# Short convolutions of a hybrid DeltaNet block: the sigmoid goes into the copied block, squares are summed on ScalarE, the halo comes from PSUM

## The chip, the cores and the metric

The kernel runs on one core of one Trainium2 chip. The metric is the device time of one execution in microseconds (us), the median of three runs. Five engines work beside each other, each through its own instructions in order: PE (TensorE, the matmuls; PEld is its weight loading), DVE (VectorE), ACT (ScalarE), POOL (GpSimd) and SP (SyncE, which issues nearly all DMAs). They wait for each other by semaphores.

## The reference

One layer of a hybrid encoder on x of 2048 tokens by 1024 channels, all in float32. One input projection feeds a gated DeltaNet (branch A) and stick-breaking attention (branch B); both are projected up, gated, merged and projected out. The change touches branch A's short causal convolution and the L2 norms of q and k:

```python
proj = jnp.einsum('bsd,dp->bsp', xn, w_in)                   # xn: RMS-normalised x
qkv_a = silu(_causal_dwconv(proj[..., :A_QKV1], conv_w))     # 4 taps along the tokens, per channel
q_a = _l2n(qkv_a[..., :nqk]...)                              # x * rsqrt(sum(x*x) + EPS), 4 heads of 128
k_a = _l2n(qkv_a[..., nqk:2*nqk]...)
v_a = qkv_a[..., 2*nqk:]
o_a = _gated_delta_rule(q_a, k_a, v_a, g, beta)              # chunks of 64 tokens, 128x128 states
...
o_b = _stick_breaking(q_b, k_b, v_b)                         # strictly causal, 8 heads of 64
merged = gates_a * (o_a @ w_up_a) + gates_b * (o_b @ w_up_b)
return x + merged @ w_out
```

## The kernel before

The projection runs unit by unit: a unit is a group of columns of w_in, for all tokens. Weights and normalised x are both held as a rounded part and a remainder (whi, wlo and xh, xl), and a product takes three matmuls per 128-row slice of the 1024 inputs, so 24 matmuls of 128x512 make one block of 128 channels by 512 tokens (`mm_chan`, L384 to L394). The block lies in PSUM under the name pj; there are four such banks.

The units come in this order: the gate path z of branch A, then the convolutions, then the projections of branch B with the triangular solves in between, then attention among the remaining projections, and the recurrence and the output products at the end. The stage of the convolutions is the stretch from about 124 to 490 us. It has four units of q and k, one per head, and two units of v. A q/k unit runs over four groups of 512 tokens, and in each over k's block and q's block (s = 0 and 1; called a pair below): 16 pairs. The v units have 16 blocks, one after the other.

Each block passes through `conv` (L534). ACT copies it from PSUM to a tile u of 515 columns (L542), whose first three columns are the last three of the block before (the halo, L541; zeros at the start, L539). DVE takes the halo for the next block (L544), multiplies the block by one tap (L546, a TENSOR_SCALAR) and adds the other three taps with three SCALAR_TENSOR_TENSOR in place on acc (L548). ACT makes the sigmoid of acc in a tile sg (L550), and POOL multiplies acc by sg, into kq for q and k (L565) or in place for v (L631).

Three steps after a pair, `qk_tok` (L572) follows it up: PE transposes k's and q's chunks to PSUM tiles tp (L582), ACT squares each of them to a tile sq (L584), DVE sums the squares by row (L585) and copies k's transposed tile (tk, L588), and a few small operations make the norms (L591 to L599, partly on POOL). POOL builds two masked tiles gm (L578), PE multiplies them to the sums of the decay exponents, ACT takes their Exp in a tile e (L605), and POOL masks e and makes en from it (L606, L610). One step later `gram` (L608) has PE make the products of k with k and q, and DVE multiplies them by en and e (L616, L617). The sigmoid and Exp need different function tables on ACT, hence the ACT_TABLE_LOADs on L550 and L605.

All tiles named u, acc, sg, gm, sq, tk, e and en come from one ring of seven buffers (tag "a", `self.na`, L212): a new tile takes the buffer of the tile seven allocations earlier and waits until its readers are done. The next unit's weights arrive in halves: ACT rounds a half (L329) and POOL takes the remainder (L330).

The program is written in the order of the loops, but a scheduler with its own timeline places the instructions of each engine, so what stands in front of what on an engine is not seen in the source.

Of the kernel before, what the change touches and what calls it, by code (L numbers as in the profile page):

```python
# [9 lines left out]
BF16 = mybir.dt.bfloat16  # L10
F32R = mybir.dt.float32r
I32 = mybir.dt.int32
AF = mybir.ActivationFunctionType
ALU = mybir.AluOpType
AX = mybir.AxisListType
# [3 lines left out]
P = 128  # L19
# [4 lines left out]
TG = 512  # L24
NG = S // TG
NH = 4
# [11 lines left out]
class Block:  # L38
# [156 lines left out]
    def stage1(self):  # L195
# [9 lines left out]
        with ExitStack() as ctx:  # L205
            with ExitStack() as early:
                self.pj = early.enter_context(self.pool("pj", bufs=4, space=PSUM))
                self.pt = early.enter_context(self.pool("pt", bufs=4, space=PSUM))
                self.wp = early.enter_context(self.pool("wp", side="right"))
                self.wcols, self.nraw = 264, 1  # L210
                with self.pool("wka", side="right") as self.wk:
                    self.na, self.nb = 7, 5  # L212
                    self.prep = self.prep_x(za[0][1])
                    next(self.prep)
                    self.units(za + conv, sb[0])
                    self.flush()
                self.wk = early.enter_context(self.pool("wkb", side="right"))
                self.na, self.nb = 8, 1
                with self.pool("sv", side="right") as self.sv:
                    self.back, self.credit = self.dn_solve(), 0.0  # L220
                    self.rate = 2.7
                    self.units(sb[:-1], sb[-1])
                    self.drain()
                wide = self.wp
                self.wp = ctx.enter_context(self.pool("wpc"))
                self.wcols = P
                self.units(sb[-1:], zb[0])
                self.flush()
# [305 lines left out]
    def conv(self, ps, b, halo):  # L534

        nc = self.nc
        u = self.a([P, TG + 3], "u")
        if halo is None:
            nc.vector.memset(u[:, 0:3], 0.0)  # L539
        else:  # L540
            nc.vector.tensor_copy(u[:, 0:3], halo)  # L541
        nc.scalar.copy(u[:, 3:], ps)  # L542
        halo = self.wk.tile([P, 3], F32, tag="halo", name="halo", bufs=4)
        nc.vector.tensor_copy(halo, u[:, TG:TG + 3])  # L544
        acc = self.a([P, TG], "acc")
        nc.vector.tensor_scalar(acc, u[:, 3:], self.tap(3, b), None, ALU.mult)  # L546
        for k in range(3):
            nc.vector.scalar_tensor_tensor(acc, u[:, k:k + TG], self.tap(k, b), acc, ALU.mult, ALU.add)  # L548
        sg = self.a([P, TG], "sg")
        nc.scalar.activation(sg, acc, AF.Sigmoid)  # L550
        return acc, sg, halo

# [19 lines left out]
    def qk_tok(self, kq, tg, h):  # L572

        nc, wk = self.nc, self.wk
        cs = slice(4 * tg, 4 * tg + 4)
        gm = [self.a([P, 4, P], "gm", F32R) for _ in range(2)]
        for t, g in zip(gm, (self.g_hi, self.g_lo)):
            nc.gpsimd.tensor_tensor(t, self.tri_le.unsqueeze(1).to_broadcast([P, 4, P]), self.col(g, tg, h).to_broadcast([P, 4, P]), ALU.mult)  # L578
        for s, ssq in ((0, self.ssq_k), (1, self.ssq_q)):
            pt = self.pt.tile([P, 4, P], F32, tag="tp", name="tp")  # L580
            for c in range(4):
                self.tr(pt[:, c], kq[:, c, s], self.ident)  # L582
            sq = self.a([P, 4, P], "sq")
            nc.scalar.activation(sq, pt, AF.Square)  # L584
            nc.vector.tensor_reduce(self.col(ssq, tg, h), sq, AX.X, ALU.add)  # L585
            if s == 0:
                tk = self.a([P, 4, P], "tk")
                nc.vector.tensor_copy(tk, pt)  # L588
                nc.sync.dma_start(self.d_kt[cs, :, h].rearrange("c p d -> p c d"), tk)
        v = wk.tile([P, 2, 4, 1], F32, tag="nv", name="nv")  # L590
        nc.vector.tensor_scalar(v[:, 0], self.col(self.ssq_k, tg, h), EPS, None, ALU.add)  # L591
        nc.vector.tensor_scalar(v[:, 1], self.col(self.ssq_q, tg, h), EPS, None, ALU.add)
        r = wk.tile([P, 4, 1], F32, tag="nr", name="nr")
        nc.vector.reciprocal(r, v[:, 0])
        nbr = self.col(self.nbr, tg, h)
        nc.vector.scalar_tensor_tensor(nbr, r, -1.0, self.col(self.beta, tg, h), ALU.mult, ALU.mult)
        nc.vector.tensor_tensor(self.col(self.nbe, tg, h), nbr, self.col(self.ed, tg, h), ALU.mult)
        nc.gpsimd.tensor_tensor(self.col(self.nk, tg, h), v[:, 0], self.half[:, 0:4].unsqueeze(2), ALU.pow)
        nc.gpsimd.tensor_tensor(self.col(self.rq, tg, h), v[:, 1], self.mhalf[:, 0:4].unsqueeze(2), ALU.pow)  # L599

        ps = self.pt.tile([P, 4, P], F32, tag="tp", name="tp")
        for k in (1, 0):
            self.mm(ps.rearrange("p c i -> p (c i)"), self.tri_gt, gm[k].rearrange("p c i -> p (c i)"), start=k == 1, stop=k == 0)
        e = self.a([P, 4, P], "e")
        nc.scalar.activation(e, ps, AF.Exp)  # L605
        nc.gpsimd.affine_select(e, e, pattern=[[0, 4], [1, P]], compare_op=ALU.is_ge, fill=0.0, base=0, channel_multiplier=-1)  # L606

        def gram():  # L608
            en = self.a([P, 4, P], "en")
            nc.gpsimd.tensor_tensor(en, e, nbr.to_broadcast([P, 4, P]), ALU.mult)  # L610
            for c2 in range(2):
                ps = self.pt.tile([P, 2, 2, P], F32, tag="tp", name="tp")
                cc = slice(2 * c2, 2 * c2 + 2)
                for c in range(2):
                    self.mm(ps[:, c], kq[:, 2 * c2 + c, 0], kq[:, 2 * c2 + c], start=True, stop=True)
                nc.vector.tensor_tensor(en[:, cc], ps[:, :, 0], en[:, cc], ALU.mult)  # L616
                nc.vector.tensor_tensor(e[:, cc], ps[:, :, 1], e[:, cc], ALU.mult)  # L617
            nc.sync.dma_start(self.d_mt[cs, h].rearrange("c j i -> j c i"), en)
            nc.sync.dma_start(self.d_qk[cs, :, h].rearrange("c j i -> j c i"), e)

        self.defer(1, gram)
# [499 lines left out]
```

## Time and profile before

| | |
|---|---|
| median of three runs | 2125.48 us (2123.26 to 2127.56) |
| the profiled execution | 2125.88 us, of which 2124.2 us is the span from the first to the last instruction |
| busy over the span | PE 2057.2 us (97%), PEld 1826.7 (86%), DVE 1408.6 (66%), ACT 878.0 (41%), POOL 932.3 (44%) |
| granted TensorE clock, mean | 0.994 |
| the chain that ended last | PE 37%, DVE 5%, DMA 4%, ACT 2%, issue 2%, POOL 1% |

PE is busy nearly all the time, so the places where it is not are what other engines cost. Matmuls are pipelined: a 128x512 matmul is shown with some 0.4 us, while such matmuls start 0.23 us apart. A row of the timeline that has a bracket at its end tells how long the engine had been idle before the instruction and what it was waiting for.

### The profile page before, as it was taken

How to read it: one execution, taken by the hardware profiler on the slowest of the kernel's cores; microseconds unless marked ns; L12 is line 12 of the kernel's file. 1: busy time of each engine (PE TensorE's matmuls, PEld its weight loads, DVE VectorE, ACT ScalarE, POOL GpSimd, SP SyncE). 2: the span in 40 equal slices, each digit the busy share in tenths (PEclk: the TensorE clock that was granted, in tenths of full speed). 3: DMA queues.
4: the chain of work that ended last, by engine and by line, in shares of the span. 5: the costliest groups of instructions: out<-in, count | busy, mean ns of one | idle time of the engine just before them, and what ended most of it. 6: DMA issues, size and time to landing. Idle time of an engine off the chain costs nothing.

```text
span 2124.2 us, 36554 instructions
## 1 busy us (share of the span) xinstructions
PE 2057.2 (97%) x12903; PEld 1826.7 (86%) x12903; DVE 1408.6 (66%) x2579; ACT 878.0 (41%) x1695; POOL 932.3 (44%) x1140
## 2 busy tenths in 40 slices
PE   8999988999999999999999999999999999999999
PEld 7988766779999988888888888888888899999887
DVE  7357787887998418887888887778744466433221
ACT  6233344322222116666666666766633321211110
POOL 4336666633443105555555554555537555521000
PEclk9999999999999999999999999999999999999999
DMA  7223333226333653444574443333346787764442
GB/s 240 63 63 95 95 95 94 85 70 120 105 120 101 159 147 103 114 117 118 148 185 122 130 122 100 109 110 108 97 133 211 234 264 220 228 189 137 152 139 80
DMA packets 279702, 282.52 MB, mean 133 GB/s; under 512 B 49440, under 2 KB 215520, under 8 KB 279392
## 3 DMA queue, kind: packets, MB, share of 16 engines
q1 hardware_dynamic: 279520, 280.19, 45.1%
q8 instruction: 103, 1.69, 0.3%
q14 instruction: 79, 0.65, 0.1%
HBM read 177.35 MB, written 102.76 MB: 132 GB/s over the span
## 4 chain that ended last, share of the span: by engine, by line
PE 37%; DVE 5%; DMA 4%; ACT 2%; issue 2%; POOL 1%; SPq 0%; DVEq 0%; ACTq 0%; POOLq 0%
PE pj L124 9%; PE o L124 8%; PE y L124 7%; PE dn L124 4%; PE av L124 3%; PE at L128 3%; DVE r L1068 2%; PE z L124 2%; DMA wraw<-in_w_in_dram 2%; DVE lo L1088 1%; ACT z L1066 1%; ACT s L1065 1%; DMA raw<-in_w_out_dram 0%; POOL xl L880 0%; DMA raw<-in_w_up_a_dram 0%
## 5 line engine op out<-in xcount | busy, mean ns | idle before, releaser
L1072 POOL TENSOR_TENSOR s<-s,r 128x512 f32<-128x512 f32 (+2 forms) x320 | 306.1, 957 | 336.8 <-DVE r L1068 330.6
L124 PE MATMUL pj<-xh,whi 128*128 128x512 f32 x1024 | 421.4, 411 | 12.2 <-ACT u L542 10.3
L124 PE MATMUL pj<-xh,wlo 128*128 128x512 f32 x1024 | 405.7, 396 | 0.0
L124 PE MATMUL pj<-xl,whi 128*128 128x512 f32 x1024 | 405.3, 396 | 0.0
L124 PE MATMUL pj<-whi,xh 128*128 128x256 f32 (+1 forms) x1024 | 294.4, 288 | 0.9 <-ACT xh L380 0.9
L124 PE MATMUL pj<-whi,xl 128*128 128x256 f32 (+1 forms) x1024 | 290.7, 284 | 0.0
L124 PE MATMUL pj<-wlo,xh 128*128 128x256 f32 (+1 forms) x1024 | 290.5, 284 | 0.2 <-DVE wlo L330 0.2
L1068 DVE TENSOR_TENSOR_SCAN r<-z,carry,zero 128x512 f32<-128x512 f32 x192 | 245.8, 1280 | 65.7 <-ACT z L1066 60.3
L124 PEld LDWEIGHTS pj<-xh,whi 128*128 128x128 f32 x1024 | 194.2, 190 | 49.4 <-ACT u L542 15.1
L124 PEld LDWEIGHTS pj<-xh,wlo 128*128 128x128 f32 x1024 | 193.7, 189 | 44.6
L1065 ACT ACTIVATE s<-z 128x512 f32<-128x512 f32 (+2 forms) x320 | 171.4, 536 | 133.4 <-PE z L124 53.6
L124 PEld LDWEIGHTS pj<-xl,whi 128*128 128x128 f32 x1024 | 194.6, 190 | 31.8
L1088 DVE TENSOR_TENSOR lo<-at,hi 128x512 fp32r<-128x512 f32 (+1 forms) x288 | 182.8, 651 | 27.2 <-ACT hi L1087 25.9
L124 PEld LDWEIGHTS pj<-whi,xh 128*128 128x128 f32 x1024 | 195.4, 191 | 1.3 <-ACT xh L380 1.3
L124 PEld LDWEIGHTS pj<-wlo,xh 128*128 128x128 f32 x1024 | 195.6, 191 | 0.5 <-DVE wlo L330 0.5
L124 PEld LDWEIGHTS pj<-whi,xl 128*128 128x128 f32 x1024 | 195.0, 191 | 0.3 <-DVE xl L381 0.3
L124 PE MATMUL z<-kt,qt 128*128 128x512 f32 (+3 forms) x640 | 189.0, 376 | 0.4 <-DVE r L1068 0.2
L1087 ACT CAST hi<-at 128x512 fp32r<-128x512 f32 (+1 forms) x288 | 154.0, 566 | 85.0 <-PE at L128 82.5
L330 POOL TENSOR_TENSOR wlo<-wraw,whi 128x512 fp32r<-128x512 f32 (+2 forms) x66 | 116.5, 1765 | 129.6 <-ACT whi L329 127.4
L1066 ACT ACTIVATE z<-z 128x512 f32<-128x512 f32 (+2 forms) x320 | 170.8, 534 | 0.1
L548 DVE SCALAR_TENSOR_TENSOR acc<-u,cols,acc 128x512 f32<-128x512 f32 x144 | 154.6, 1073 | 5.0
L128 PE MATMUL at<-ident,s 128*128 128x128 f32 x1088 | 155.6, 275 | 1.8 <-POOL s L1072 1.4
(200 smaller groups left out, 4285.3 us busy)
## 6 DMA issues: line engine op xcount, KB each, us to landing
kt<-d_k SPq DMA_DIRECT2D x160, 128.0 KB, 3.0
vt<-d_v SPq DMA_DIRECT2D x80, 256.0 KB, 3.6
xt<-in_x_dram SPq DMA_DIRECT2D x32, 512.0 KB, 3.6
qt<-d_q SPq DMA_DIRECT2D x64, 256.0 KB, 5.4
d_g<-sg SPq DMA_DIRECT2D x128, 128.0 KB, 2.5
gt<-d_g SPq DMA_DIRECT2D x64, 256.0 KB, 3.5
wraw<-in_w_in_dram SPq DMA_DIRECT2D x56, 256.0 KB, 3.3
wraw<-in_w_in_dram SPq DMA_DIRECT2D x18, 512.0 KB, 3.9
```

Source lines behind the costliest of these rows:

```text
L124: self.pin(self.nc.tensor.matmul(out, lhsT, rhs, **kw))
L128: self.pin(self.nc.tensor.transpose(*args))
L330: (eng or nc.gpsimd).tensor_tensor(lo[:, ks, :n], raw[:, :, :n], hi[:, ks, :n].bitcast(F32), ALU.subtract)
L548: nc.vector.scalar_tensor_tensor(acc, u[:, k:k + TG], self.tap(k, b), acc, ALU.mult, ALU.add)
L1065: nc.scalar.activation(s[:, :w], z[:, :w], AF.Sigmoid, scale=SD ** -0.5)
L1066: nc.scalar.activation(z[:, :w], z[:, :w], AF.Sigmoid, scale=-(SD ** -0.5))
L1068: nc.vector.tensor_tensor_scan(r[:, 0:w][:, ::-1], z[:, 0:w][:, ::-1], self.zero.to_broadcast([P, w]), init, ALU.mult, ALU.add)
L1072: nc.gpsimd.tensor_mul(s[:, :w], s[:, :w], r[:, 1:w + 1])
L1087: nc.scalar.copy(hi[:, c:], flat[:, c:])
L1088: nc.vector.tensor_tensor(lo[:, c:], flat[:, c:], hi[:, c:].bitcast(F32), ALU.subtract)
```

## The change

Three edits, all in `conv` and `qk_tok`. The sigmoid is written over the first 512 columns of u, so that sg no longer takes a buffer of the ring. The halo for the next block is copied from the block in PSUM and no longer from u. And each transposed tile is squared chunk by chunk, four ACT operations of 128x128, whose row sums go to the norm's columns directly; the squares themselves go to a bfloat16 tile sink that nobody reads. The tile sq and DVE's two sums fall away. The ring serves 9 tiles per pair and no longer 13.

```diff
@@ conv
         nc.scalar.copy(u[:, 3:], ps)
         halo = self.wk.tile([P, 3], F32, tag="halo", name="halo", bufs=4)
-        nc.vector.tensor_copy(halo, u[:, TG:TG + 3])
+        nc.vector.tensor_copy(halo, ps[:, TG - 3:TG])
...
-        sg = self.a([P, TG], "sg")
+        sg = u[:, 0:TG]
         nc.scalar.activation(sg, acc, AF.Sigmoid)
@@ qk_tok
-            sq = self.a([P, 4, P], "sq")
-            nc.scalar.activation(sq, pt, AF.Square)
-            nc.vector.tensor_reduce(self.col(ssq, tg, h), sq, AX.X, ALU.add)
+            junk = wk.tile([P, P], BF16, tag="sink", name="sink", bufs=1)
+            for c in range(4):
+                n = NH * (4 * tg + c) + h
+                nc.scalar.activation(junk, pt[:, c], AF.Square, accum_out=ssq[:, n:n + 1])
```

The scheduler places the instructions anew in the whole stage. On ACT, one round of a q/k pair in the middle of the stage stands like this before (u are the copied blocks, sg the sigmoids, e the Exp):

```order
L542 COPY u<-pj 128x512
L550 ACT_TABLE_LOAD
L550 ACTIVATE sg<-acc 128x512
L542 COPY u<-pj 128x512
L550 ACTIVATE sg<-acc 128x512
L584 ACTIVATE sq<-tp 128x512 x2
L605 ACT_TABLE_LOAD
L605 ACTIVATE e<-tp 128x512
L542 COPY u<-pj 128x512
```

And like this in the changed kernel, where a line below the edit has a number that is one higher:

```order
L542 COPY u<-pj 128x512 x2
L586 ACTIVATE sink,ssq_k<-tp 128x128 x3
L550 ACT_TABLE_LOAD
L550 ACTIVATE u<-acc 128x512
L586 ACTIVATE sink,ssq_k<-tp 128x128
L586 ACTIVATE sink,ssq_q<-tp 128x128 x4
L550 ACTIVATE u<-acc 128x512
L606 ACT_TABLE_LOAD
L606 ACTIVATE e<-tp 128x512
L542 COPY u<-pj 128x512
```

Both blocks of a pair are now copied ahead of both sigmoids; before, the second copy stood behind the first sigmoid. The squares moved from behind the second sigmoid to places ahead of it.

On DVE, this is the second block of a pair and what follows it up, before:

```order
L544 COPY halo<-u 128x3
L546 TENSOR_SCALAR acc<-u,cols 128x512
L548 SCALAR_TENSOR_TENSOR acc<-u,cols,acc 128x512 x3
L585 TENSOR_REDUCE ssq_k<-sq 128x4
L588 COPY tk<-tp 128x512
L585 TENSOR_REDUCE ssq_q<-sq 128x4
L591 TENSOR_SCALAR nv<-ssq_k 128x4
L592 TENSOR_SCALAR nv<-ssq_q 128x4
L594 RECIPROCAL nr<-nv 128x4
L541 COPY u<-halo 128x3
L596 SCALAR_TENSOR_TENSOR nbr<-nr,beta 128x4
L597 TENSOR_TENSOR nbe<-nbr,ed 128x4
```

And in the changed kernel:

```order
L544 COPY halo<-pj 128x3
L546 TENSOR_SCALAR acc<-u,cols 128x512
L592 TENSOR_SCALAR nv<-ssq_k 128x4
L548 SCALAR_TENSOR_TENSOR acc<-u,cols,acc 128x512
L595 RECIPROCAL nr<-nv 128x4
L548 SCALAR_TENSOR_TENSOR acc<-u,cols,acc 128x512
L597 SCALAR_TENSOR_TENSOR nbr<-nr,beta 128x4
L593 TENSOR_SCALAR nv<-ssq_q 128x4
L589 COPY tk<-tp 128x512
L548 SCALAR_TENSOR_TENSOR acc<-u,cols,acc 128x512
L598 TENSOR_TENSOR nbe<-nbr,ed 128x4
```

The follow-up moved in between the taps of the second block, as the operations on en and e did between the taps of the first. Outside the stage of the convolutions the order is the same but for a few neighbours that changed places on DVE in the solves.

## Rows read from the trace of the kernel before

**Rows 1.** Busy time by stretch: length, PE, PEld, DVE, ACT, POOL, clock, DMA, GB/s.
```profile
153.00:410.00 257.00, 238.68 (x1060) 189.35 (x1059) 200.87 (x361) 104.19 (x145) 162.79 (x129) 0.99 0.31 94
410.00:490.00 80.00, 75.41 (x377) 61.48 (x376) 67.93 (x111) 23.75 (x38) 31.22 (x23) 0.98 0.27 78
```
**Rows 2.** Waits from 153 to 410 us: who for whom, us, times, longest.
```profile
PE pj L124 <- ACT u L542: 10.3, 11, 2.5
...
PE tp L128 <- ACT e L605: 6.6, 11, 1.1
```
**Rows 3.** Timeline of ACT over a pair without weights: start, us, instruction, idle before.
```profile
258.02 0.63 ACT L550 ACTIVATE sg<-acc 128x512 f32<-128x512 f32 x1 [5.08 <-DVE acc L548]
258.56 1.06 ACT L584 ACTIVATE sq<-tp 128x512 f32<-128x512 f32 x2
259.94 1.28 ACT L605 ACT_TABLE_LOAD   x1 [0.31 <-DVE ssq_k L585]
...
261.73 0.58 ACT L542 COPY u<-pj 128x512 f32<-128x512 f32 x1
266.26 1.28 ACT L550 ACT_TABLE_LOAD   x1 [3.96 <-DVE u L539]
...
268.10 0.56 ACT L542 COPY u<-pj 128x512 f32<-128x512 f32 x1
273.78 0.64 ACT L550 ACTIVATE sg<-acc 128x512 f32<-128x512 f32 x1 [5.12 <-DVE acc L548]
```
**Rows 4.** Timeline of ACT: the first and the last second-block sigmoid of the q/k units.
```profile
153.12 0.63 ACT L550 ACTIVATE sg<-acc 128x512 f32<-128x512 f32 x1 [5.30 <-DVE acc L548]
...
408.88 0.63 ACT L550 ACTIVATE sg<-acc 128x512 f32<-128x512 f32 x1 [5.08 <-DVE acc L548]
```
**Rows 5.** PE's groups by line, 153 to 410 us: one of three kinds of products.
```profile
L124 PE MATMUL pj<-xh,wlo 128*128 128x512 f32 x263 | 105.1, 399 | 0.0
```
**Rows 6.** Timeline of ACT over a pair with weights.
```profile
289.50 0.63 ACT L550 ACTIVATE sg<-acc 128x512 f32<-128x512 f32 x1 [5.09 <-DVE acc L548]
...
302.69 1.05 ACT L329 CAST whi<-wraw 128x1024 fp32r<-128x1024 f32 x1
309.90 0.63 ACT L550 ACTIVATE sg<-acc 128x512 f32<-128x512 f32 x1 [6.16 <-DVE acc L548]
```
**Rows 7.** Timeline of DVE over the pair of Rows 3.
```profile
259.78 0.68 DVE L588 COPY tk<-tp 128x512 f32<-128x512 f32 x1
...
262.34 0.17 DVE L544 COPY halo<-u 128x3 f32<-128x3 f32 x1 [0.59 <-ACT u L542]
...
262.93 3.25 DVE L548 SCALAR_TENSOR_TENSOR acc<-u,cols,acc 128x512 f32<-128x512 f32 x3
...
264.76 1.43 DVE L548 SCALAR_TENSOR_TENSOR acc<-u,cols,acc 128x512 f32<-128x512 f32 x1
266.12 0.41 DVE L616 TENSOR_TENSOR en<-tp,en 128x256 f32<-128x256 f32 x1
...
268.69 0.90 DVE L544 COPY halo<-u 128x3 f32<-128x3 f32 x1 [1.17 <-ACT u L542]
...
270.02 3.67 DVE L548 SCALAR_TENSOR_TENSOR acc<-u,cols,acc 128x512 f32<-128x512 f32 x3
```
**Rows 8.** Timeline of POOL over the same pair.
```profile
268.27 1.30 POOL L565 TENSOR_TENSOR kq<-acc,sg 128x512 f32<-128x512 f32 x1 [2.63 <-ACT sg L550]
```
**Rows 9.** All taps of the three-operand form: ns min, median, max, first and last start.
```profile
L548 DVE SCALAR_TENSOR_TENSOR acc<-u,cols,acc x144: 739/753/2780, 130.0 to 486.3; 128x512 f32<-128x512 f32 x144
```
**Rows 10.** ACT operations by line: ns min, median, max, first and last start.
```profile
L370 ACT ACTIVATE junk<-xt x16: 1049/1059/1082, 4.3 to 59.3; 128x1024 bf16<-128x1024 f32 x16
L370 ACT ACTIVATION_READ_ACCUMULATOR junk<-xt x16: 185/193/219, 5.3 to 60.3; 128x1 f32 x16
...
L475 ACT ACTIVATE egc<-tp x1: 223/223/223, 143.0 to 143.0; 128x64 f32<-128x64 f32 x1
L584 ACT ACTIVATE sq<-tp x32: 577/584/597, 153.7 to 410.8; 128x512 f32<-128x512 f32 x32
```

## The prediction

> **What bounds the kernel now.** I read the page's chain first: PE has 37% of it and no other engine over 5%, so the end of the kernel is set by when PE gets through its work, and a change elsewhere counts only where it lets PE run. The stretches then show where PE stands still around the edits. From 153 to 410 us, the q/k pairs, PE is busy 238.68 of 257.00 us, from 410 to 490, the v blocks, 75.41 of 80.00 [rows 1]. That is 18.3 and 4.6 us of idle time. The granted clock is 0.99 and 0.98 there, so PE lost another 257 x 0.01 + 80 x 0.02 = 4.2 us to spells at the lower of its two levels, which come after stalls. Together 27.1 us: no edit in this stage can give more, and behind it the order hardly changes and PE carries on at its own speed, so what is won here should arrive at the end.
>
> The waits name the cause: PE waits for a free bank (for the copy u) and for the Exp e, about once per pair each [rows 2]. Both are ACT's, and ACT itself waits: in a pair without weights it stands 3.96 us and 5.12 us for DVE's taps [rows 3]. So the stage is a ring between ACT and DVE: copy, taps, sigmoid, next copy, taps, sigmoid, squares, Exp, copy. Its period is 273.78 - 258.02 = 15.76 us. A pair that also rounds weights takes 309.90 - 289.50 = 20.40 us [rows 6], 4.64 more, and there are 4 of those among the 15 periods from the first to the last [rows 4], which last 408.88 - 153.12 = 255.8 us together.
>
> PE needs less. There are three groups of pj products like the one shown, 262 + 263 + 262 = 787, or 787/24 = 32.8 blocks, 16.4 pairs, in 238.68 us [rows 1, 5]: 14.55 us per pair with all that belongs to it, 218 us for 15. The ring is 37 us too slow for that over its 15 periods. PE shows only half of it as idle time since it fills its free banks meanwhile, and lives on that lead among the v blocks.
>
> **The change part by part, per pair.** ACT: two squares of 128x512 go (0.53 us each, 1.06 for both [rows 3]), eight of 128x128 with a row sum come. No row shows such a one. The line through 223 ns for 64 columns and 584 ns for 512 gives 0.27 us for 128, and the only row sums in the trace add an own instruction of 0.19 us [rows 10]: 0.47 us, and about 0.5 as each waits for the one before it. Bounds: 0.22 us (64 columns, no sum) and 1.25 us (1059 + 193 ns, 1024 columns) [rows 10]. I take 0.5, by the 64-column row, which is the nearest in size: eight cost 4.0 us, and ACT gets 2.9 us more to do. It is hidden: ACT has those 3.96 and 5.12 us of waiting in every pair, and the new order puts the squares there, ahead of the sigmoids instead of behind them. Behind them they were in the ring.
>
> The ring itself gets shorter, since both blocks of a pair are copied at once. The second copy no longer waits for the first sigmoid, and DVE goes from the first block to the second without ACT in between. What is left on ACT per round, between the last tap and the next halo: sigmoid 0.54 (258.02 to 258.56), table 1.28, Exp 0.51 (259.94 + 1.28 to 261.73), copy 0.61 (261.73 to the halo at 262.34) [rows 3, 7]: 2.94 us. Gone from it are a table load, a sigmoid, a copy, the two squares and the 0.31 us for the ring's buffer.
>
> DVE per round: the first block 262.34 to 266.12, 3.78 us; the second 268.69 to the sigmoid at 273.78, 5.09; four products with en and e, 4 x 0.41 = 1.64 (one shown); tk 0.68; four small ones and a halo put into u, 5 x 0.17 = 0.85 by the shorter halo copy, which has as few columns [rows 3, 7]. Sum 3.78 + 5.09 + 1.64 + 0.68 + 0.85 = 12.0 us. The two row sums on DVE are gone. With ACT 12.0 + 2.94 = 14.9 us, if nothing else changes.
>
> The halo from PSUM: in this pair the two halo copies took 0.17 and 0.90 us. The second started at 268.69 while POOL multiplied from 268.27 to 269.57, and it ended when POOL did [rows 7, 8]. So a small copy from SBUF to SBUF waits for POOL here. If a copy from PSUM doesn't, 0.73 us goes and the ring is at 14.2. If the tap behind it (also SBUF to SBUF, 0.43 us from the halo's end to the next instruction) then stands where the halo stood, it stays at 14.9. The Trainium skill, "SBUF — State Buffer", section "Who interferes with whom", states that rule: copies and tensor_scalar in their two-port form and a GpSimd operation exclude each other for a whole instruction, and an operation with at most one SBUF input outside that form is free. By it the halo is freed and the tap waits in its place, which is the case of 14.9 below; the trace agrees on the halo, and no row shows a halo from PSUM. I take the middle, 14.5 us.
>
> That is just under PE's 14.55, so pairs without weights run at PE's speed. Pairs with weights: the first rounding now stands between the two copies, while DVE is at the first block, and drops out of the ring (1.05 us, as the other one [rows 6]); the second one and POOL's work stay: 14.5 + 4.64 - 1.05 = 18.1 us.
>
> Waits added: a bank of pj now comes free only after DVE's halo too. In the new order PE is at most two blocks ahead of the copy, and there are four banks, so nothing is queued behind that. The tile u is held until POOL has multiplied, but the ring of buffers serves 9 tiles per pair and no longer 13. DVE's sum of q's norm waits for the last four squares; by 0.5 us each they end 0.54 + 2.0 us after the first block's last tap, when DVE is still at the second block.
>
> **The sum.** Ring over 15 periods: 11 x 14.55 + 4 x 18.1 = 232.5 us, 23 less than before. PE needs 218; 14.3 us too much remain. The new order lets PE run about one block ahead, half a pair, 7.3 us. Idle left among the pairs: 14.3 - 7.3 = 7.0. Among the v blocks, where the ring is faster than PE (it has the same operations as before), I leave half of the 4.6, and half of the 4.2 of clock. Left 7.0 + 2.3 + 2.1 = 11.4 of 27.1; won 15.7. The profiled execution took 2125.88 us: 2110.2. The median of the runs shown, 2125.48, is 0.4 us off that and changes nothing.
>
> **The rivals.**
> *The wait only moves* to the tap: normal pairs 14.9, with weights 18.5, ring 11 x 14.9 + 4 x 18.5 = 238. Idle 238 - 218 - 7.3 = 12.7, and 2.3 + 2.5 beside it: 9.6 won, 2116. For it: the tap has the same kind of operands as the halo had. Against it: it waits in few pairs now.
> *All idle time goes:* the ring falls well below PE also with weights. 2125.9 - 27.1 = 2099, by half of the pieces left 2101. Against it: POOL's weights still take DVE's time.
> *No change.* The six three-operand taps took 3.25 + 3.67 = 6.9 us in this pair, the last of the first three 1.43 alone, while the median over all of them is 753 ns [rows 7, 9]. I take POOL's work beside them for the cause, as with the halo. If the denser DVE order puts all six beside POOL, they take 6 x 1.43 = 8.6 us. Ring 14.2 + 1.7 = 15.9, where it was: 2126. The section of the Trainium skill named above also has an operation with two SBUF inputs, as these taps are, shut out by a GpSimd operation that reads SBUF; the trace shows them slowed. For it: POOL has the same work in a shorter round. Against it: it is four tenths idle even now (162.79 of 257.00 [rows 1]).
> *Slower:* the squares on ACT. Four stand ahead of the first sigmoid. Two copies, four squares of p us and a table load, 1.14 + 4p + 1.28, have to fit in the 5.4 us of DVE's first block with its products (3.78 + 1.64), so above p = 0.75 us each further 0.1 makes the round 0.4 longer. Four more stand ahead of the second sigmoid and DVE's last tap, with 4.4 us of room, so from p = 1.1 that comes twice. The gain of 1.26 us per pair is used up at p = 1.06. At the upper bound of 1.25 us: 2.0 + 0.65 = 2.65 us per pair, ring 17.2 and 20.8, 15 x 1.44 - 4 x 1.04 = 17 us longer: 2143. Against it: the columns are an eighth of that row's.
>
> **How the numbers follow.** Forecast 2110, chance 0.40, by itself 2104 to 2115; the wait moves, 0.18; all idle time goes, 0.07; no change, 0.23; slower, by the squares or by taps slowed still more, 0.12. A measurement of this kernel can tell 0.2%, 4.3 us, from no change, so faster is below 2121.2. The first three cases are, and a tenth of the fourth: 0.67. Of the rest 0.21 is within 0.2%, 0.12 slower. The range leaves out the slower case and half of the best one: 2100 to 2128.
>
> **What would show it.** Right: PE's idle time between 153 and 410 us falls from 18 to about 7 us; the period of pairs without weights is 14.5 to 14.9 us; the stage of the convolutions ends some 15 us earlier; a square takes 0.5 us with its sum; halo copies take 0.17 us throughout; ACT's wait for taps stays its longest. Wrong: pairs that stay near 15.8 us, taps that are all at 1.4 us, ACT's squares on the way to a sigmoid that DVE no longer holds up, or a PE that waits elsewhere, as for POOL's gm ahead of the Exp.

## The result, and the profile after

The changed kernel takes 2099.07 us (median of 4 runs, 2097.94 to 2102.16), the kernel before on the same chip 2124.37: a ratio of 0.9882, 95% interval 0.9870 to 0.9894, or 25.3 us less. The forecast was 2110, its range began at 2100. What came is close to the rival in which all idle time goes, 2099.

The profiled execution took 2102.16 us, 23.7 less than that of before. The whole gain lies in the stage of the convolutions. Its last sigmoid starts at 463.05 us and no longer at 487.13, 24.1 us earlier, and 463 to 2100 us takes as long as 487 to 2124 took.

Stretches of the changed kernel, in the columns of [rows 1]:

```profile
153.00:410.00 257.00, 249.68 (x1150) 203.97 (x1148) 184.59 (x375) 142.46 (x369) 175.65 (x139) 0.99 0.33 101
410.00:490.00 80.00, 80.00 (x504) 71.53 (x503) 52.04 (x91) 16.91 (x27) 26.95 (x17) 1.00 0.48 99
```

PE's idle time fell from 18.3 to 7.3 us and from 4.6 to 0. PE's waits between 124 and 490 us are now these (for whom, us in total, times, longest):

```profile
PE tp L124 <- DVE nbr L597: 2.6, 1, 2.6
PE tp L124 <- DVE nv L593: 2.4, 1, 2.4
PE tp L128 <- ACT e L606: 1.6, 1, 1.6
PE tp L124 <- POOL gm L578: 0.5, 1, 0.5
PE tp L128 <- POOL kq L565: 0.2, 1, 0.2
```

The two rows of [rows 2] are gone or reduced to one wait: no copy u holds PE any more. What is left are five single waits, all in pairs that round weights.

ACT over a pair without weights, which answers to [rows 3]:

```profile
202.01 0.63 ACT L550 ACTIVATE u<-acc 128x512 f32<-128x512 f32 x1 [2.54 <-DVE acc L548]
202.65 1.28 ACT L606 ACT_TABLE_LOAD   x1
203.95 0.60 ACT L606 ACTIVATE e<-tp 128x512 f32<-128x512 f32 x1
204.44 0.58 ACT L542 COPY u<-pj 128x512 f32<-128x512 f32 x1
206.11 0.59 ACT L542 COPY u<-pj 128x512 f32<-128x512 f32 x1 [1.09 <-POOL e L607]
206.60 0.28 ACT L586 ACTIVATE sink<-tp 128x128 bf16<-128x128 f32 x1
206.77 0.20 ACT L586 ACTIVATION_READ_ACCUMULATOR sink<-tp 128x1 f32 x1
207.00 0.28 ACT L586 ACTIVATE sink<-tp 128x128 bf16<-128x128 f32 x1
...
210.62 0.63 ACT L550 ACTIVATE u<-acc 128x512 f32<-128x512 f32 x1 [1.15 <-DVE acc L548]
...
215.57 0.63 ACT L550 ACTIVATE u<-acc 128x512 f32<-128x512 f32 x1 [2.86 <-DVE acc L548]
```

The second copy starts at 206.11, 4.5 us ahead of the first sigmoid; before it came behind it. This holds for 13 of the 16 pairs: in the first three the second copy still stands behind the first sigmoid. The pair takes 215.57 - 202.01 = 13.56 us. A square with its row sum starts 0.40 us after the one before it (206.60 to 207.00). Over all 15 periods, the second-block sigmoids run from 153.55 to this one:

```profile
377.83 0.63 ACT L550 ACTIVATE u<-acc 128x512 f32<-128x512 f32 x1 [1.85 <-DVE acc L548]
```

That is 224.3 us, 14.95 each on average, against 255.8 before [rows 4].

DVE from 153 to 410 us by kind (count, busy us, mean ns, idle time ahead), first of before:

```profile
L548 DVE SCALAR_TENSOR_TENSOR acc<-u,cols,acc 128x512 f32<-128x512 f32 x91 | 111.4, 1224 | 3.2
L544 DVE COPY halo<-u 128x3 f32<-128x3 f32 x30 | 17.9, 596 | 32.3 <-ACT u L542 32.3
L546 DVE TENSOR_SCALAR acc<-u,cols 128x512 f32<-128x512 f32 x30 | 16.1, 536 | 0.0
```

And after:

```profile
L548 DVE SCALAR_TENSOR_TENSOR acc<-u,cols,acc 128x512 f32<-128x512 f32 x106 | 101.7, 959 | 0.9
L546 DVE TENSOR_SCALAR acc<-u,cols 128x512 f32<-128x512 f32 x36 | 25.3, 703 | 0.0
L541 DVE COPY u<-halo 128x3 f32<-128x3 f32 x28 | 15.3, 545 | 1.2 <-DMA d_kt<-tk 1.2
```

Three things are to be seen. A three-operand tap takes 959 ns on average and no longer 1224. The halo copy of 596 ns is out of the list (below). And two others have become longer: the first tap, 536 to 703 ns, and the copy of the halo into u, now 545.

### The profile page after: what moved, and what is told of

It reads as the page before. It is cut to its first block, busy times and chain, and to the rows that moved or that the text cites. A ratio compares the mean times of both kernels' runs of the same rounds, so it can differ in the third digit from the quotient of the medians.

```text
span 2100.5 us, 36701 instructions
## 1 busy us (share of the span) xinstructions
PE 2045.1 (97%) x12903; PEld 1822.8 (87%) x12903; DVE 1360.8 (65%) x2547; ACT 909.3 (43%) x1919; POOL 935.3 (45%) x1140
## 4 chain that ended last, share of the span: by engine, by line
PE 38%; DVE 4%; DMA 4%; ACT 2%; issue 2%; POOL 1%; SPq 1%; DVEq 0%; ACTq 0%; POOLq 0%
PE pj L124 10%; PE o L124 8%; PE y L124 7%; PE dn L124 4%; PE av L124 3%; PE at L128 3%; PE z L124 3%; DVE r L1069 2%; DMA wraw<-in_w_in_dram 2%; DVE lo L1089 1%; DMA ot<-d_ob 1%; ACT z L1067 1%; ACT s L1066 1%; DMA raw<-in_w_out_dram 1%; DMA gt<-d_g 0%
## 5 line engine op out<-in xcount | busy, mean ns | idle before, releaser
L124 PE MATMUL av<-lo,vt 128*128 128x256 f32 x576 | 147.3, 290 | 9.2 <-DVE lo L1089 4.3
```

The source lines that it names most:

```text
L124: self.pin(self.nc.tensor.matmul(out, lhsT, rhs, **kw))
```

## Experiments

Two theories were put against each other. A: the new order does it, since both copies stand ahead of both sigmoids and DVE goes from one block to the next without ACT. B: the work that leaves DVE does it, edit by edit. The table has all kernels but the two with shorter products, which come below (one run each, 2112.99 and 2068.67 us). Idle is PE's, from the busy time of the two stretches in the profiled execution. The runs of before beside them had medians of 2124.4 to 2126.3 us; differences between kernels of different rows are taken from the ratios, times 2125 us.

| kernel | us | ratio to before, 95% interval | idle 153 to 410 | idle 410 to 490 |
|---|---|---|---|---|
| halo_only | 2122.18 | 0.9988 (0.9979 to 0.9998) | 16.8 | 2.3 |
| sigmoid_only | 2109.23 | 0.9924 (0.9911 to 0.9937) | 13.9 | 0 |
| sums_only | 2117.11 | 0.9958 (0.9945 to 0.9971) | 10.1 | 4.2 |
| no_halo_edit | 2104.10 | 0.9905 (0.9892 to 0.9918) | 10.9 | 0 |
| no_sums_edit | 2102.87 | 0.9894 (0.9880 to 0.9907) | 10.1 | 0 |
| no_sigmoid_edit | 2109.36 | 0.9927 (0.9913 to 0.9941) | 8.0 | 2.3 |
| all three | 2099.07 | 0.9882 (0.9870 to 0.9894) | 7.3 | 0 |
| four_buffers | 2142.03 | 1.0074 (1.0062 to 1.0087) | 21.3 | 4.8 |
| five_buffers_after | 2117.28 | 0.9962 (0.9950 to 0.9973) | 13.1 | 6.1 |
| nine_buffers_after | 2116.34 | 0.9952 (0.9940 to 0.9964) | 15.8 | 0 |
| nine_buffers_before | 2129.28 | 1.0018 (1.0009 to 1.0027) | 18.3 | 5.5 |
| four_weight_buffers_before | 2126.18 | 1.0005 (0.9996 to 1.0013) | 19.7 | 4.2 |
| copies_first_before | 2104.64 | 0.9896 (0.9879 to 0.9913) | 5.8 | 3.8 |
| copies_first_nine_before | 2108.75 | 0.9920 (0.9907 to 0.9932) | 5.2 | 4.7 |
| squares_twice | 2123.18 | 0.9981 (0.9973 to 0.9990) | 22.5 | 0 |
| masks_first | 2108.95 | 0.9922 (0.9906 to 0.9937) | 12.3 | 0 |
| masks_first_squares_twice | 2121.85 | 0.9983 (0.9973 to 0.9992) | 20.4 | 0 |

### One edit at a time, and all but one

Each kernel takes one, two or all three hunks of the diff shown above; halo_only for instance is

```diff
-        nc.vector.tensor_copy(halo, u[:, TG:TG + 3])
+        nc.vector.tensor_copy(halo, ps[:, TG - 3:TG])
```

**halo_only.** 

> Only the halo is copied from PSUM; all engines keep the order of the kernel before. Theory A (the new order does it: the sigmoid over u leaves the ring of buffers shorter of work, so both copies stand ahead of both sigmoids and DVE need not wait for ACT inside a pair): the halo copies fall to 0.16 us, but the wait for POOL goes partly to the tap and to the copy u<-halo; 2114 to 2122 us, 2118 taken. Theory B (less work on DVE does it, and each edit gives what it takes off DVE): halo copies of 0.60 us mean become 0.15, 0.9 us per pair, 14 us over 16 pairs: 2108 to 2114. If the wait for POOL only moves: 2122 to 2127.

Measured 2122.18, 0.12% less than before: just above A's 2114 to 2122, at the lower edge of the case in which the wait moves. The halo copies do fall to one length, and the first tap takes over. By line over the whole kernel (ns min, median, max), before and then halo_only:

```profile
L544 DVE COPY halo<-u x48: 154/873/2301, 129.5 to 482.0; 128x3 f32<-128x3 f32 x48
...
L546 DVE TENSOR_SCALAR acc<-u,cols x48: 473/476/1527, 129.5 to 484.2; 128x512 f32<-128x512 f32 x48
```

```profile
L544 DVE COPY halo<-pj x48: 147/160/163, 129.4 to 478.5; 128x3 f32<-128x3 f32 x48
...
L546 DVE TENSOR_SCALAR acc<-u,cols x48: 476/1052/2493, 129.5 to 478.6; 128x512 f32<-128x512 f32 x48
```

No halo copy waits any more, but the median first tap goes from 476 to 1052 ns. This is the case that the forecast had at 14.9 us per pair. PE's wait keeps its size and only changes its name, as the bank is now released by the halo copy:

```profile
PE pj L124 <- DVE halo L544: 10.0, 11, 2.5
```

The Trainium skill, "SBUF — State Buffer", section "Who interferes with whom", has this: operations with at most one SBUF input outside the two-port form are free of GpSimd, two-port copies and tensor_scalar are not. This trace agrees on the halo, 147 to 163 ns from PSUM, and on the tap, which now waits in its place (median 1052 ns).

**sigmoid_only.** 

> Only the sigmoid is written over u; squares and row sums as before, halo from u. ACT's order becomes copy, copy, sigmoid, squares, sigmoid. Theory A: most of the gain, 2101 to 2107 us, and PE's wait for ACT's copy u is gone. Theory B: DVE's work is the same, so 2118 to 2126.

Measured 2109.23: 16 us, between the two, nearer to A. PE's wait for the copy u is gone, and so is all idle time among the v blocks.

**sums_only.** 

> Only the squares with row sums on ACT; the second copy still stands behind the first sigmoid. Theory A: 2114 to 2122 us, as the two reduces (0.68 us each) and the squares leave the ring but DVE still waits for the second copy. Theory B: 1.37 us per pair leave DVE, 22 us over 16 pairs: 2103 to 2109.

Measured 2117.11, in A's range; B had 2103 to 2109.

**no_halo_edit, no_sums_edit and no_sigmoid_edit** give the other cells.

> Sigmoid over u and sums on ACT, halo still from u: the changed kernel without one edit; the order on ACT is that of the changed kernel. Theory A: DVE has some 3 us of slack per pair, which hides 0.9 us of halo: 2098 to 2102 us, not to be told from the changed kernel. Theory B: the halo's 14 us come back in part: 2105 to 2112.

> Sigmoid over u and halo from PSUM; squares and their sums as before, on DVE. If the three edits add up: 2125.3 less 16.1 (sigmoid) less 3 to 4 (halo): 2105 to 2107 us. If the halo only pays where DVE is short of work: 2108 to 2110, as sigmoid_only. If the sums on DVE hide the halo's gain in a stall: above 2110.

> Halo from PSUM and sums on ACT; the sigmoid keeps its tile in the ring, so the second copy stands behind the first sigmoid as in sums_only. If the edits add up: 2117 less 3 to 4: 2113 to 2114 us, and the v blocks keep their 4 us of idle time. If the halo's wait only moves to the tap: 2117.

Measured 2104.10, 2102.87 and 2109.36. The first lies between the two theories, the other two below all that was expected. So the edits neither simply add up nor cover each other. The halo, worth 2.6 us alone, is worth 6.4 beside the sigmoid edit and 6.6 beside the sums. The sums are worth 8.9 alone, but on top of the other two only 2.6, less than the intervals can tell. The sigmoid edit is the largest everywhere, 9.6 to 20 us.

### The ring by itself

In the convolutions two of the three products per slice remain, so PE no longer covers the ring of ACT and DVE:

```diff
-            for n, (a, b) in enumerate(((hi, self.xh[tg]), (hi, self.xl[tg]), (lo, self.xh[tg]))):
+            for n, (a, b) in enumerate(((hi, self.xh[tg]), (lo, self.xh[tg]))):
```

> The kernel before with two in place of three products per slice in the convolutions (the product with the remainder of x is left out there), so PE needs some 11 us per pair and the ring of ACT and DVE stands free. If a ring sets the pace before, its period stays at 15.4 to 15.8 us for pairs without weights and some 20 with. If PE's products set it, it falls to 12 to 14.

> The changed kernel with two in place of three products per slice in the convolutions, so that its ring shows. By the working of the forecast 14.5 us without weights, 18.1 with. By the trace of the changed kernel, where DVE is busy 170.85 us in 16 pairs, 10.7 each, and waits for ACT 2.9 us: 12.5 to 13.6 without weights, 15 to 17 with.

Second-block sigmoids of the kernel before with short products:

```profile
251.79 0.63 ACT L552 ACTIVATE sg<-acc 128x512 f32<-128x512 f32 x1 [5.11 <-DVE acc L550]
...
267.50 0.64 ACT L552 ACTIVATE sg<-acc 128x512 f32<-128x512 f32 x1 [5.08 <-DVE acc L550]
...
283.22 0.63 ACT L552 ACTIVATE sg<-acc 128x512 f32<-128x512 f32 x1 [5.09 <-DVE acc L550]
```

15.71 and 15.72 us, with a third of the products gone: in pairs without weights the ring sets the pace before, as read from [rows 3]. The "some 20 with" did not come: from the fourth pair on, the pairs that round weights took 15.7 to 16.3 us, but for one of 19.6. So the 20.4 us of [rows 6] are not the ring's own length; more on them below. The changed kernel with short products:

```profile
180.78 0.63 ACT L552 ACTIVATE u<-acc 128x512 f32<-128x512 f32 x1 [2.16 <-DVE acc L550]
...
193.29 0.63 ACT L552 ACTIVATE u<-acc 128x512 f32<-128x512 f32 x1 [0.91 <-DVE acc L550]
...
207.91 0.63 ACT L552 ACTIVATE u<-acc 128x512 f32<-128x512 f32 x1 [2.81 <-DVE acc L550]
...
225.18 0.63 ACT L552 ACTIVATE u<-acc 128x512 f32<-128x512 f32 x1 [4.66 <-DVE acc L550]
...
237.73 0.63 ACT L552 ACTIVATE u<-acc 128x512 f32<-128x512 f32 x1 [0.90 <-DVE acc L550]
```

12.5 and 14.6 us without weights, 17.3 with, then 12.6. The forecast had 14.5 and 18.1: too long by about 1 us, and not of one length. All 15 periods together take 221.6 us, hardly less than the 224.3 with all products. So the changed kernel's ring is by itself about as long as with PE's full work beside it, as far as this can be told: the scheduler placed the squares otherwise here.

### Buffers or order

The sigmoid edit does two things: it frees buffers of the ring, and the scheduler puts the second copy first. These kernels change the number of buffers (`self.na`) alone in the source; the scheduler places the instructions anew for each. In the changed kernel:

```diff
-                    self.na, self.nb = 7, 5
+                    self.na, self.nb = 4, 5
```

with 5 in place of 4 in five_buffers_after, and 9, 4 in nine_buffers_after and nine_buffers_before.

> The changed kernel with a ring of four buffers in place of seven in this stage: nine tiles per pair go round it 2.25 times, thirteen in seven buffers 1.86 times before. On ACT the second copy stands behind the first sigmoid again, the squares stay ahead. Theory A (the sigmoid over u helps because fewer tiles share the ring, so copies are not held up): the share that sigmoid_only won is lost, 2112 to 2122 us, PE waits for ACT's copy u again and stands idle among the v blocks. Rival (the place of the sigmoid itself does it, by less work beside each other): 2098 to 2105.

> The changed kernel with five buffers: 1.8 rounds per pair, as deep as before (1.86), but both copies stay ahead of both sigmoids. If buffers as such set the pace: the share of sigmoid_only is lost, 2112 to 2120 us. If the place of the second copy does it: 2099 to 2104.

> The changed kernel with nine buffers in the ring and four for kq and weights: exactly one round per pair. If buffers still hold it up: POOL's waits for the DMA of en (17 us) and PE's 7 us of waits go, 2092 to 2096 us. If ACT, DVE and PE are balanced by now: 2098 to 2103.

> The kernel before with nine buffers in the ring in place of seven (and four in place of five for kq and incoming weights, to make room): thirteen tiles go round 1.44 times per pair, 1.86 before, 1.29 in the changed kernel. In the order the second copy still stands behind the first sigmoid. If buffers as such hold up the pace: 2112 to 2118 us, a good half of sigmoid_only's 16. If the place of the second copy in the order does it: 2122 to 2127, as before.

> The kernel before with four in place of five buffers for kq and incoming weights, the ring of seven as it was: what the room for the nine buffers costs by itself. 2124 to 2128 us if nothing waits for those buffers; up to 2135 if weights come later.

Fewer buffers cost 41 and 17 us against the changed kernel (of the 41, some 10 lie ahead of the convolutions, whose first copy starts at 139.06 us and not at 128.62). Four came above both ranges; five, at 2117.28, came in the range for buffers and not in that for the order. With five the order of the copies holds, but DVE now waits for buffers (the first row) and PE stands among the v blocks again (the second), so the order of the copies alone doesn't carry the gain when buffers are short:

```profile
DVE u L541 <- POOL kq L565: 19.3, 9, 2.2
```

```profile
PE tp L128 <- POOL acc L632: 6.0, 7, 1.4
```

More buffers did not help either: 2129.28 for before, whose order they leave as it was, and 2116.34 for the changed kernel, 15 us worse, where the scheduler now put the second copy behind the first sigmoid in 9 of the 16 pairs (three in the changed kernel). The control for the room, 2126.18, can't be told from before. So neither expectation held for nine buffers in the changed kernel, and in both the time went with the order. (The 17 us of waiting named there are masks_first's, below; the changed kernel has 2.0.) The last pair changes that order in the source, and no work, tile or buffer: both sigmoids of a pair, and POOL's products that need them, are written behind both copies (`conv` with False leaves its own sigmoid out), sg keeps its tile, halo and sums stay. In the trace 15 of the 16 pairs have this order; what stands around it, on DVE above all, the scheduler moved with it.

```diff
-                acc, sg, halo[s] = self.conv(ps, h + NH * s, halo[s])
-                nc.gpsimd.tensor_tensor(kq[:, :, 1 - s], acc..., sg..., ALU.mult)
+                acc, sg, halo[s] = self.conv(ps, h + NH * s, halo[s], False)
+                both.append((acc, sg))
                 if s == 0:
                     self.step()
+            for s, (acc, sg) in enumerate(both):
+                nc.scalar.activation(sg, acc, AF.Sigmoid)
+                nc.gpsimd.tensor_tensor(kq[:, :, 1 - s], acc..., sg..., ALU.mult)
```

> The kernel before with one thing changed: both sigmoids of a pair are written behind both copies, so ACT's order is copy, copy, sigmoid, sigmoid, squares, Exp; sg keeps its tile, the ring its seven buffers, halo and sums are as before. If the order of the copies is what the sigmoid's edit gives: 2108 to 2116 us. If it needs the free buffers as well: 2117 to 2125. If neither: 2125 or more.

> The same order with nine buffers in the ring (1.44 rounds per pair) and four for kq and weights. If order and buffers are what the sigmoid's edit gives: 2106 to 2112 us, as sigmoid_only's 2109. If it is the place of the sigmoid itself: 2122 to 2130, as nine_buffers_before.

2104.64 us with seven buffers, below its range for the order alone; 2108.75 with nine. None of the three edits is in it, and yet it wins 22 of the 25 us. Its stretches, in an execution of 2111.40 us, the longest of five:

```profile
153.00:410.00 257.00, 251.19 (x1144) 205.03 (x1143) 195.72 (x388) 110.77 (x153) 159.49 (x135) 0.99 0.33 99
410.00:490.00 80.00, 76.25 (x455) 65.96 (x454) 59.35 (x98) 17.51 (x29) 27.61 (x19) 0.98 0.46 95
```

Between 153 and 410 us PE idles 5.8 us, less than in the changed kernel; among the v blocks, where this order can't apply, the 3.8 us stay. The 15 periods take 240.1 us, against 255.8 before and 224.3 in the changed kernel. So the ring is shortened by half as much, and PE's idle time in this stretch is not the ring's alone. How the order shortens the ring is seen on DVE, in one round, and on POOL beside it:

```profile
207.47 0.16 DVE L544 COPY halo<-u 128x3 f32<-128x3 f32 x1
207.54 0.48 DVE L546 TENSOR_SCALAR acc<-u,cols 128x512 f32<-128x512 f32 x1
...
209.93 2.85 DVE L548 SCALAR_TENSOR_TENSOR acc<-u,cols,acc 128x512 f32<-128x512 f32 x4
```

```profile
213.39 1.29 POOL L571 TENSOR_TENSOR kq<-acc,sg 128x512 f32<-128x512 f32 x1 [6.53 <-ACT sg L570]
```

Four taps in 2.85 us, 0.71 each, and a halo from SBUF that takes 0.16. I read it so: POOL's products wait for the sigmoids, and those stand behind the taps, so POOL (idle for 6.53 us here, while the taps ran) works while DVE has other things to do. From 153 to 410 us a tap takes 913 ns on average here and 1224 before.

### Squares and POOL's queue

Here each square was made twice in the changed kernel, as a test of the claim that ACT's squares are hidden:

```diff
+                for _ in range(2):
                     nc.scalar.activation(junk, pt[:, c], AF.Square, accum_out=ssq[:, n:n + 1])
```

> The changed kernel with every square and its row sum made twice (the sums are unchanged): ACT gets 8 more of 0.40 us, 3.2 us per pair. Theory A (PE sets the pace, ACT waits 77 us for DVE in 235 us, 4.8 per pair): hidden but for 0 to 0.5 us per pair, 2099 to 2106 us. Rival (squares stand on the path to the first sigmoid): 3.2 us per pair less the slack of some 1.5, 16 x 1.7 = 27 us: 2115 to 2130.

2123.18, the rival: 21 us by the ratios for 16 x 3.2 us of ACT work. The squares are not covered beyond what they take now. But the work did not change alone: the scheduler put the second copy behind the first sigmoid in six pairs (three in the changed kernel) and, in most, squares between the second sigmoid and the Exp. The 21 us are those of both. The waits that grew:

```profile
PE tp L124 <- POOL gm L578: 17.4, 12, 2.7
```

```profile
DVE nv L594 <- ACT sink L587: 22.4, 14, 3.0
```

From these I formed theory C: nv is late, POOL's nk waits for nv, and gm stands behind nk. The test orders nk behind both gm tiles (`mask` is the second of them):

```diff
+        self.tc.add_manual_dep(nk.ins, mask.ins.name, ...)
```

> The changed kernel with POOL's power nk ordered behind both masked tiles gm of its pair; nothing else is touched. Theory C (what holds PE in the changed kernel, and what made squares_twice slow, is POOL's queue: nk waits for DVE's nv, nv for the last square, gm stands behind nk, and PE needs gm): the three stalls at gm, 0.5, 2.6 and 2.4 us, go with some 0.3 us hidden beside each: about 6 us less than the changed kernel, 2091 to 2096 us. Rival (ACT and DVE set this pace whatever POOL's order): 2098 to 2102.

> The same, and every square with its row sum made twice (sums unchanged). Theory C: of the 24 us that doubling the squares cost, PE's 17.4 us of waiting for gm go: 2100 to 2110 us. Rival (eight more ACT operations per pair lengthen the ring of ACT and DVE by themselves): 2117 to 2124.

2108.95 and 2121.85. The second kernel is no test: ACT, DVE and POOL have the same order in it as in squares_twice throughout the stage, and 2121.85 is that kernel's time over again. But that order answers the question by itself, as nk stands behind both gm there without being told to. In one pair of squares_twice:

```profile
327.58 1.63 POOL L565 TENSOR_TENSOR kq<-acc,u 128x512 f32<-128x512 f32 x1 [3.41 <-ACT u L550]
329.28 1.38 POOL L578 TENSOR_TENSOR gm<-tri_le,g_lo 128x512 fp32r<-128x512 f32 x1
331.10 1.44 POOL L600 TENSOR_TENSOR nk<-nv,half 128x4 f32<-128x4 f32 x1 [0.44 <-DVE nv L593]
```

So with doubled squares theory C falls. The second gm is late because it stands behind POOL's product kq, which waits for a late sigmoid, and in four pairs because it waits for a buffer of the ring:

```profile
POOL gm L578 <- DMA d_mt<-en: 16.8, 4, 4.8
```

That is how the doubled squares reach PE as far as the trace shows it; no run takes this path away. In the changed kernel theory C did not come true either: with nk behind both gm it gets 8.5 us slower. But here too the order changed elsewhere: the second copy stands behind the first sigmoid in six pairs, and gm waits 17.7 us for buffers, 2.0 in the changed kernel. What the place of nk alone is worth stays open.

## Why the prediction was too high

**Right: what bounds the kernel.** The ring of ACT and DVE sets the pace before in pairs without weights; short_products_before shows it at 15.7 us with a third of PE's products gone. That PE's idle time falls from 18 to about 7 us among the pairs is what was measured, 7.3, but by luck (below). That the second copy's place shortens the ring is shown by copies_first_before (15 periods in 240.1 us), and its 22 us of time are more than I had put on it.

**Wrong: the ceiling.** "Together 27.1 us: no edit in this stage can give more" fails: what was won stayed under it, but not for its reason, as the sum took PE's busy time as fixed. By the same rows of after, 7.3 us of idle time and 257 x 0.01 = 2.6 us of clock are left, 9.9 of the 27.1, so 17.2 us would have been won. The profiled executions differ by 23.7. The rest is in PE's busy time. From the first copy u to the last one, the same blocks pass through PE; the stretch before, and after:

```profile
127.87:481.38 353.51, 331.21 (x1495) 263.43 (x1493) 283.45 (x506) 133.16 (x192) 197.55 (x154) 0.99 0.29 87
```

```profile
128.62:456.80 328.18, 320.86 (x1483) 262.27 (x1482) 238.42 (x474) 163.89 (x415) 199.84 (x154) 0.99 0.31 94
```

Idle time falls by 15.0 us, from 22.3 to 7.3, and busy time by 10.35. Some 1.4 us of that are 12 short matmuls of the next unit (an estimate: half of the 0.23 us between matmuls of 512 columns). Another 1.5 us are the clock: before, PE was busy for 6.4 us of this stretch at the lower of its two levels (granted clock 0.50, at 302 and 371 us, around the ends of two stalls of 2.5 us), after for 3.4 us (at 378 us, behind a stall of 2.4 us); half of the difference is lost time. A matmul is shown with 0.4 us though the next starts 0.23 us later, so ahead of every stall some 0.17 us of standing still count as busy, and a shorter stall doesn't show at all. The trace of before has 31 stalls of PE here, that of after 5. Taking each matmul's time to the next start beyond the median of its kind, outside the spells at the lower clock, gives 9.4 us before and 2.1 after: 7.3 us that no row of idle time had. Of these the 26 stalls that are gone explain 26 x 0.17 = 4.4 by themselves. With the 1.4 and the 1.5 that makes 10.2 of the 10.35. It is read from the traces; no experiment isolates it.

**Wrong: the ring's size.** The 15 periods were put at 232.5 us and took 224.3. DVE's round was put at 12.0 us, while DVE is busy 10.7 us per pair (170.85 us for the 16 pairs, 153 to 388 us). Its taps were those of one pair of before, 6.9 us for six; they take 6 x 0.96 = 5.8, as fewer stand beside POOL. The four products were counted at 0.41 us each, the length that is shown, but start 0.33 us apart (at 235.61 and 235.94 us in the changed kernel). The first taps and the copies into u, which became longer, take a part of this back. The squares came at 0.40 us and not 0.5.

The extra 4.64 us of pairs with weights were misread. The forecast took 1.05 us of ACT's rounding out of them and left the rest in the ring, 18.1 us; with short products it was 17.3. In the pair of [rows 6], the taps and POOL's remainders of the weights stood like this:

```profile
295.05 5.27 DVE L548 SCALAR_TENSOR_TENSOR acc<-u,cols,acc 128x512 f32<-128x512 f32 x3
...
304.13 5.68 DVE L548 SCALAR_TENSOR_TENSOR acc<-u,cols,acc 128x512 f32<-128x512 f32 x3
```

```profile
294.63 2.65 POOL L330 TENSOR_TENSOR wlo<-wraw,whi 128x1024 fp32r<-128x1024 f32 x1
...
303.82 2.52 POOL L330 TENSOR_TENSOR wlo<-wraw,whi 128x1024 fp32r<-128x1024 f32 x1
```

The six taps take 10.95 us, 4.0 more than the 3.25 + 3.67 of the pair without weights [rows 7]. So 4.0 of the 4.64 were taps slowed beside POOL, and only 0.6 the rounding. How long such a pair is depends on what stands beside what, hence 15.7 to 16.3 us in short_products_before.

That the idle time left is still the forecast 7.0 comes from two errors that cancel: the ring is 8.2 us shorter, and the lead of 7.3 us that I gave PE isn't there (224.3 - 218 = 6.3, near the measured 7.3).

**Wrong: half of the rest.** Of the v blocks' 4.6 us I left 2.3; none is left. It goes with the sigmoid's edit: all kernels that have it and at least seven buffers have 0 there, and all with sg in the ring 2.3 to 5.5. The buffer that sg gives back is not shown as the cause, since nine buffers with sg in the ring still have 5.5 and 4.7; how the edit does it stays open.

**The rivals.** That the wait only moves to the tap is what the halo edit does alone, but with the new order it moves to the tap and to u's halo, and the halo edit is still worth 4.9 us on top of the other two (0.9905 to 0.9882). "Slower by the squares" didn't come, but its threshold missed something: I had 0.75 us each before the first cost, and doubling them to 0.80 us cost 1.3 us per pair, where my working gives 0.2. The changed order has a share in that, and the path from a late sigmoid over POOL's products and gm to PE, which the working leaves out.

## What to carry to other kernels

Between two engines that hand blocks to each other, look first at the order on the engine that serves both: taking in the second block before finishing the first won here 22 of the 25 us that three edits did, with no change in work or buffers. More buffers were no gain by themselves: nine in place of seven cost 15 us where they changed the order that the scheduler found, and 4 where they did not; fewer cost 17 and 41. Where a scheduler places the instructions, compare the orders of two kernels before laying their difference to the edit: one test here changed no order at all, and another changed far more than was meant. And idle time of a pipelined engine is a lower bound on what stalls cost: count the stalls too, and compare busy time over the same work.

## What was not expected of the hardware

- A 128x128 square with a row sum starts every 0.40 us: 278 ns for the operation and 194 ns for the reading of the sum, which overlap by some 0.07 us.
- A copy of 128x3 from PSUM took 142 to 163 ns in all 48 cases; from SBUF it took up to 2301 ns.
- Taps with three operands took 739 to 2780 ns before and 733 to 2777 after: the same bounds. From 153 to 410 us their mean fell from 1224 to 959 ns in the changed kernel, and to 913 by order alone (copies_first_before).
